# A hybrid layer on one core: when the conditioning products run in the mixer, and narrower products in the first feed-forward block

## The chip, the cores and the metric

One core of one Trainium2 chip runs the whole layer in one launch. The metric is the time on the device of one execution. The kernel before took 543.53 us (median of 3 runs, 543.39 to 544.7). The profiled execution took 542.25 us, of which the profile's span covers 540.5 us.

## The reference

One decoder layer on 256 tokens with 1024 features, in float32. The input x passes a SwiGLU feed-forward block, a mixer and a second feed-forward block, each with a normed and modulated input and a gated residual, and a last norm.

```
mod = (c @ w_ada + b_ada).reshape(B, 9, 1024)
sh1, sc1, g1, sh2, sc2, g2, sh3, sc3, g3 = [mod[:, None, i] for i in range(9)]
h = rmsnorm(x, ffn1_norm) * (1 + sc1) + sh1
x = x + 0.5 * (1 + g1) * swiglu(h, ffn1_w_gate, ffn1_w_up, ffn1_w_down)
h = rmsnorm(x, mix_norm) * (1 + sc2) + sh2
x = x + (1 + g2) * hybrid_mixer(h, ...)
h = rmsnorm(x, ffn2_norm) * (1 + sc3) + sh3
x = x + 0.5 * (1 + g3) * swiglu(h, ffn2_w_gate, ffn2_w_up, ffn2_w_down)
return rmsnorm(x, final_norm)
```

swiglu(h) is (silu(h @ w_gate) * (h @ w_up)) @ w_down with a hidden width of 2816. The mixer projects h to q, k, v of an attention with 8 heads, to x_m for a stabilised mLSTM with 4 heads (in the reference in chunks of 64 tokens), and to a gate z. It norms both results, multiplies the mLSTM's by silu(z), and multiplies the two, side by side, by w_out. The nine vectors of mod are the conditioning: 9 x 1024 sums over 1024 elements, one for each feature and kind.

## The kernel before, in words

Features lie on the partitions and the 256 tokens along the free axis. A product in float32 is made from two parts of each operand: `hi` is the value rounded to TensorE's fp32r format, `lo` the remainder. `mm3` issues three matmuls of 256 columns (258 where two columns for the shift are carried along): hi by hi, lo weight by hi, hi weight by lo. Weights come in pieces of 1 MB (`raw`, 4 buffers); ScalarE (ACT) makes `whi` of a piece by a cast, VectorE (DVE) makes `wlo` by a subtraction, each in two halves of 1024 columns. `weights()` hands out one piece, asks for the one three ahead, and splits the next.

The conditioning is not made by TensorE. For each of the 72 rows of 128 features `ada` loads 512 KB (3 buffers) and DVE multiplies it by c and sums along the row: one `scalar_tensor_tensor`, called `junk` in the trace after its unused output. `side(...)` is called at fixed places and takes one such job from the list `jobs` for each of its arguments. After the first feed-forward block 22 jobs are left for the mixer: 6 for the mixer's gate, 8 for the scale of the third norm and 8 for its shift.

The work goes in this order. The first feed-forward block makes gate and up until 140.5 us and the down product until about 202 us: 8 output blocks d, each over 22 pieces of the hidden width. In it, one matmul of 512 columns takes hi of a weight block against [gh|gl], the two halves of the hidden values, and a second of 256 columns takes lo against gh. The second half of the 512 lands in its own part of the PSUM tile, and DVE adds it to x with a `scalar_tensor_tensor` (`x` in the trace) of its own. The second block's down product is made in the same way for d = 0 to 6, and by `mm3` for the last d.

The mixer runs from 202 to 340 us: x_m (`px`), then pairs of column tiles in `tiles()`: queries 0 and 1, values 0, queries 2 and 3, values 1, and z twice (each 16 `mm3`, in two halves). Between the tiles stand the small pieces of attention and mLSTM. `gates` and `decays` make the mLSTM's decay matrices `wE` (DVE, from a TensorE product of `rows` with `ohr`), `m_scores(h)` makes q by k and multiplies it into `wE[h]` on DVE, `m_sums` sums over it, `m_vars` and `m_factors` make the norm (`dd`, `vv`, `rs`, `nw`, `rows`), and `z_silu` is the silu of z. Then `w_out` in 4 pieces of weights c, each for two of the eight input tiles k: k = 0 to 3 is the attention's output (`mix(0)` to `mix(3)`, split into `hh` and `hl` from `oa`), k = 4 to 7 the mLSTM's, made in `m_out`. `pre_shift(2)` makes the two shift columns for the second feed-forward block, whose gate and up run from 340 to 468 us, the down product until 529 us.

The order on each engine comes from two sources. Instructions for which `keep_in_program_order` was called (through the class `Ordered`, while its `on` is set) keep the order of the code among themselves. All others are placed by the scheduler, which plays the program with its own costs and puts each where its engine seems free. In the mixer, ACT and DVE are pinned from `weigh(3)` to `a_out`, and from `m_factors` to `m_out_pre`; the conditioning products aren't. All DMAs of weights and rows are issued by SyncE (SP), in one queue. Almost every instruction has line 55 in the trace, that of the helper.

Of the kernel before, what the change touches and what calls it, by code (L numbers as in the profile page):

```python
# [14 lines left out]
ALU = mybir.AluOpType  # L15
# [5 lines left out]
ND = 8  # L21
# [40 lines left out]
def layer(ctx: ExitStack, tc: tile.TileContext, i, out: bass.AP):  # L62
    nc = tc.nc
    act, dve, pool, pe = (Ordered(tc, e) for e in (nc.scalar, nc.vector, nc.gpsimd, nc.tensor))
# [20 lines left out]
    def bank(tag):  # L85
        return psp.tile([P, 512], F32, tag=tag, name=nm("ps" + tag), bufs=BANKS[tag])
# [38 lines left out]
    c_bc = const([P, D], F32, "c_bc")  # L125
# [115 lines left out]
    mod = const([P, 72], F32, "mod")  # L241
# [2 lines left out]
    gt = [const([P, ND], F32, f"gt{k}") for k in range(3)]  # L244
    NCOL = [C_N1, C_N2, C_N3]

    def ada(col, on_pool=False):

        t = wp.tile([P, D], F32, tag="ada", name=nm("ada"), bufs=3)
        dma(t, i["ada"][col])  # L250
        junk = wp.tile([P, D], BF16, tag="junk", name=nm("junk"), bufs=1)
        dve.scalar_tensor_tensor(junk, t, 1.0, c_bc, ALU.mult, ALU.mult,
                                 accum_out=mod[:, col:col + 1])

    def ada_gate_fin(k):
        s0 = 24 * k + 16
# [145 lines left out]
    def ffn(k, nxt):  # L402
        nfa = 3
        with tc.tile_pool(name=f"g{k}", bufs=1) as gp:
# [132 lines left out]
            for d in range(ND):  # L537
                pd = bank(ring[d % 8])
                for ft in range(NF):
                    b = d * NF + ft  # L540
                    if b % 16 == 0:
                        w = weights()
                        side(*QD[k][b // 16 % 2])
                    if nxt is None and d == ND - 1:
                        mm3(pd[:, 0:T], w, (b % 16) * P, gh[:, ft], gl[:, ft], start=(ft == 0), stop=(ft == NF - 1))
                        continue
                    hi, lo = part(w, (b % 16) * P, P)
                    pe.matmul(pd, hi, g2[:, ft], start=(ft == 0), stop=(ft == NF - 1), skip_group_check=True)
                    rest.append(lambda lo=lo, ft=ft, pd=pd: pe.matmul(
                        pd[:, 0:T], lo, gh[:, ft], start=False, stop=(ft == NF - 1), skip_group_check=True))  # L550
                    while rest and (ft < NF - 4 or ft == NF - 1):
                        rest.pop(0)()
                if nxt is not None or d < ND - 1:
                    dve.scalar_tensor_tensor(x_sb[:, d], pd[:, T:2 * T], gt[k][:, d:d + 1], x_sb[:, d], ALU.mult,
                                             ALU.add)
                nxt_sq[0] = residual(d, pd[:, 0:T], gt[k], nxt)
                if d == 6 and nxt is not None:
                    pre_shift(nxt)
# [5 lines left out]
    def side(*on):  # L564

        for o in on:
            if jobs:
                jobs.pop(0)(o)
# [5 lines left out]


    px = [bank("a") for _ in range(4)]
    for c in range(2):
        w = weights()
        side(1, 0)
        for d4 in range(4):  # L580
            d = c * 4 + d4
            for h in range(NH):
                mm3(px[h][:, 0:W], w, d4 * 512 + h * P, hh[:, d], hl[:, d], start=(d == 0), stop=(d == 7))
            if d == 0:
                r = rstd_of([acc, nxt_sq[0]], pre=False)
    with tc.tile_pool(name="mix", bufs=1) as mp:
        mixer(tc, nc, i, mp, locals())


    with tc.tile_pool(name="fin", bufs=1) as fp:  # L590
# [10 lines left out]
def mixer(tc, nc, i, mp, L):  # L601
    act, dve, pool, pe, sp = L["act"], L["dve"], L["pool"], L["pe"], L["sp"]
# [221 lines left out]
    def mix(k):  # L824
        return mix0 if k == 0 else (hh[:, k, 0:T], hl[:, k, 0:T])
# [3 lines left out]
    def z_silu(h2):  # L829
        z2 = zs[:, 2 * h2:2 * h2 + 2]  # L830
        tc.keep_in_program_order(act.activation(z2, z2, AF.Silu))
# [105 lines left out]
    conv(1)  # L937
    next(g)
    fold()
    side(1, 0)  # L940
    g = queries(1)
    conv(2)
    next(g)
    conv(3)
    next(g)
    g0 = values(0)
    side(0, 1)
    next(g0)
    gates()
    next(g0)  # L950
    scores(0)
    m_queries()
    g = queries(2)
    side(0, 1)
    next(g)
    next(g0)
    m_values()
# [2 lines left out]
    scores(1)  # L960
    turn(0)
    g = queries(3)
    side(0, 1)
    next(g)
    weigh(0)
    m_scores(0)
# [3 lines left out]
    scores(2)  # L970
    m_scores(2)
    g0 = values(1)
    side(0, 1)
    next(g0)
    weigh(1)
    scores(3)
# [3 lines left out]
    m_scores(3)  # L980
    m_sums(1)
    g = tiles(shifted(zs[:, 0]), shifted(zs[:, 1]))
    side(1, 0, 0)
    next(g)
    next(g0)
    turn(3)
# [10 lines left out]
    m_vars(1)  # L997
    m_vars(2)
    g = tiles(shifted(zs[:, 2]), shifted(zs[:, 3]))
    side(1)  # L1000
    next(g)
    m_vars(3)
    m_factors()
    z_silu(0)
    next(g)
    for j in range(1, 4):
        hilo(*mix(j), oa[:, j, 0:T])
    z_silu(1)
    for h in range(NH):
        m_out_pre(h)  # L1010
# [1 line left out]
    po = [bank(t) for t in ("m", "m", "a", "a")]  # L1012
    for c in range(4):
        w = weights()
        side(0)
        pe.on = c < 2
        for k2 in range(2):
            k = c * 2 + k2
            for d in range(8):
                mm3(po[d // 2][:, (d % 2) * T:(d % 2 + 1) * T], w, (k2 * 8 + d) * P, *mix(k),  # L1020
                    start=(c == 0 and k2 == 0 and d % 2 == 0), stop=(c == 3 and k2 == 1))
                if (k, d) == (2, 7):
                    m_spread()
                    for h in range(NH):
                        m_out(h)
    side(*[0] * len(jobs))
    L["pre_shift"](2)
    for d in range(8):
        nxt_sq[0] = residual(d, po[d // 2][:, (d % 2) * T:(d % 2 + 1) * T], L["gt"][1], 2)

# [85 lines left out]
```

## Time and profile before

| | us |
|---|---|
| time, median of 3 runs | 543.53 |
| time of the profiled execution | 542.25 |
| span of the profile | 540.5 |
| TensorE (PE) busy | 516.9 (96%), 3826 matmuls |
| VectorE (DVE) busy | 424.1 (78%) |
| ScalarE (ACT) busy | 282.6 (52%) |
| DMA | 125.73 MB, mean 233 GB/s |
| PE idle in one piece, in the mixer | 4.20 before 282.05, 0.74 before 285.74, 4.75 before 316.55 |

Busy time is the sum of the instructions of an engine, with overlaps counted once. An idle time in brackets stands ahead of the instruction that ended it, with the engine that released it. "PEclk" is the granted clock of TensorE as a share of full speed. In the chain of waits each row is one stretch of the path that ended last.

### The profile page before, as it was taken

How to read it: one execution, taken by the hardware profiler on the slowest of the kernel's cores; microseconds unless marked ns; L12 is line 12 of the kernel's file. 1: busy time of each engine (PE TensorE's matmuls, PEld its weight loads, DVE VectorE, ACT ScalarE, POOL GpSimd, SP SyncE). 2: the span in 40 equal slices, each digit the busy share in tenths (PEclk: the TensorE clock that was granted, in tenths of full speed). 3: DMA queues.
4: the chain of work that ended last, by engine and by line, in shares of the span. 5: the costliest groups of instructions: out<-in, count | busy, mean ns of one | idle time of the engine just before them, and what ended most of it. 6: DMA issues, size and time to landing. Idle time of an engine off the chain costs nothing.

```text
span 540.5 us, 9607 instructions
## 1 busy us (share of the span) xinstructions
PE 516.9 (96%) x3826; PEld 484.0 (90%) x3826; DVE 424.1 (78%) x717; ACT 282.6 (52%) x484; POOL 46.2 (9%) x60
## 2 busy tenths in 40 slices
PE   8999999999999999999969969999999999999992
PEld 7899999999988889978856869999999999988892
DVE  7899978988799988997894666979987777655433
ACT  4364456665554454648655544965554554544410
POOL 5000000000010210200010000400000000012320
PEclk9999999999999999999999979999999999999997
DMA  8999986587788985776771114387855455455002
GB/s 314 352 368 396 372 333 235 212 303 276 278 345 320 346 340 180 266 297 235 308 275 42 50 69 136 101 349 292 312 202 206 178 169 211 167 181 209 1 1 78
DMA packets 24095, 125.73 MB, mean 233 GB/s; under 512 B 2673, under 2 KB 3185, under 8 KB 14578
## 3 DMA queue, kind: packets, MB, share of 16 engines
q1 hardware_dynamic: 23762, 124.72, 61.6%
q8 instruction: 30, 0.49, 0.4%
q10 hardware_dynamic: 288, 0.39, 0.2%
q14 instruction: 15, 0.12, 0.1%
HBM read 124.05 MB, written 1.05 MB: 231 GB/s over the span
## 4 chain that ended last, share of the span: by engine, by line
PE 89%; DVE 4%; DMA 2%; ACT 2%; issue 1%; SPq 0%; DVEq 0%; ACTq 0%
PE psa L55 45%; PE psb L55 25%; PE psm L55 20%; DMA ada<-in_ada 2%; DVE junk L55 1%; ACT whi L55 1%; DVE wE L55 1%; DVE wlo L55 0%; DVE ht L55 0%; DVE u_out L55 0%; SPq L98 0%; ACT hh L55 0%; ACT L55 0%; ACT zs L55 0%; DVE nw L55 0%
## 5 line engine op out<-in xcount | busy, mean ns | idle before, releaser
L55 ACT ACTIVATE whi<-raw 128x1024 fp32r<-128x1024 f32 (+1 forms) x160 | 166.8, 1047 | 133.1 <-PE psa L55 83.4
L55 DVE TENSOR_TENSOR wlo<-raw,whi 128x1024 fp32r<-128x1024 f32 (+1 forms) x160 | 193.8, 1215 | 50.3 <-ACT whi L55 48.7
L55 PE MATMUL psa<-hh,wlo 128*128 128x256 f32 (+1 forms) x452 | 127.2, 282 | 0.0
L55 PE MATMUL psa<-hh,whi 128*128 128x256 f32 (+1 forms) x452 | 127.0, 283 | 0.0
L55 PE MATMUL psa<-hl,whi 128*128 128x256 f32 (+1 forms) x452 | 126.1, 281 | 0.0
L55 DVE SCALAR_TENSOR_TENSOR junk<-ada,c_bc 128x1024 bf16<-128x1024 f32 x72 | 89.4, 1242 | 8.3 <-DMA ada<-in_ada 7.7
L55 PEld LDWEIGHTS psa<-hh,wlo 128*128 128x128 f32 x452 | 85.9, 190 | 0.1
L55 PEld LDWEIGHTS psa<-hh,whi 128*128 128x128 f32 x452 | 85.7, 190 | 0.0
L55 PEld LDWEIGHTS psa<-hl,whi 128*128 128x128 f32 x452 | 85.5, 190 | 0.0
L55 PE MATMUL psb<-hh,whi 128*128 128x258 f32 (+1 forms) x284 | 81.6, 288 | 0.6 <-ACT whi L55 0.6
L55 PE MATMUL psb<-hh,wlo 128*128 128x258 f32 (+1 forms) x284 | 80.2, 283 | 0.6 <-DVE wlo L55 0.6
L55 PE MATMUL psb<-hl,whi 128*128 128x258 f32 (+1 forms) x284 | 79.8, 283 | 0.0
L55 PE MATMUL psa<-g,whi 128*128 128x512 f32 (+1 forms) x198 | 59.8, 369 | 0.0
L55 PEld LDWEIGHTS psb<-hh,whi 128*128 128x128 f32 x284 | 53.7, 189 | 2.7 <-issue 1.0
L55 PEld LDWEIGHTS psb<-hh,wlo 128*128 128x128 f32 x284 | 53.8, 189 | 0.9 <-DVE wlo L55 0.8
L55 PEld LDWEIGHTS psb<-hl,whi 128*128 128x128 f32 x284 | 53.5, 189 | 0.2 <-issue 0.2
L55 PE MATMUL psm<-hh,whi 128*128 128x256 f32 (+1 forms) x168 | 48.1, 287 | 4.8 <-ACT hh L55 4.8
L55 PE MATMUL psm<-hh,wlo 128*128 128x256 f32 (+1 forms) x168 | 47.8, 285 | 0.0
L55 PE MATMUL psm<-hl,whi 128*128 128x256 f32 (+1 forms) x168 | 47.5, 285 | 0.0
L55 PE MATMUL psa<-g,wlo 128*128 128x256 f32 x176 | 45.9, 281 | 0.0
L55 PEld LDWEIGHTS psa<-g,whi 128*128 128x128 f32 x198 | 35.2, 188 | 6.2
L55 PEld LDWEIGHTS psm<-hh,whi 128*128 128x128 f32 x168 | 32.5, 194 | 5.1 <-ACT hh L55 5.0
(238 smaller groups left out, 759.5 us busy)
## 6 DMA issues: line engine op xcount, KB each, us to landing
ada<-in_ada SPq DMA_DIRECT2D x72, 512.0 KB, 5.8
raw<-in_dn SPq DMA_DIRECT2D x22, 1024.0 KB, 4.8
raw<-in_guB SPq DMA_DIRECT2D x19, 1024.0 KB, 4.8
raw<-in_gu SPq DMA_DIRECT2D x18, 1024.0 KB, 6.4
raw<-in_gu SPq DMA_DIRECT2D x8, 512.0 KB, 7.3
raw<-in_wqk SPq DMA_DIRECT2D x4, 1024.0 KB, 5.4
raw<-in_wout SPq DMA_DIRECT2D x4, 1024.0 KB, 6.8
raw<-in_guA SPq DMA_DIRECT2D x4, 768.0 KB, 4.0
```

The source lines that it names most:

```text
L55: r = f(*a, **k)
```

## The change

There are five edits. While `pinned[0]` is set, from the end of the first feed-forward block to the end of the mixer, the conditioning products are kept in program order with the other pinned instructions of DVE. Their places in the mixer are dealt out anew: 2 and 1 in x_m, 2 in the first queries, one each in the five pairs of tiles that follow, 5 in the first z pair, 4 in the second, 2 and 1 in the last two pieces of w_out (before: two in each place up to values 1, then 3, 1, 1, 1). `z_silu(0)` moves behind the splits of `mix(1)` to `mix(3)`. `pre_shift(2)` is pinned on ACT and DVE. In the down product of the first feed-forward block all eight output blocks are made by `mm3`, and the DVE add of the second half falls away there; the second feed-forward block keeps the 512 columns.

```diff
+    pinned = [False]
+
     def ada(col, on_pool=False):
 
         t = wp.tile([P, D], F32, tag="ada", name=nm("ada"), bufs=3)
         dma(t, i["ada"][col])
         junk = wp.tile([P, D], BF16, tag="junk", name=nm("junk"), bufs=1)
-        dve.scalar_tensor_tensor(junk, t, 1.0, c_bc, ALU.mult, ALU.mult,
-                                 accum_out=mod[:, col:col + 1])
+        p = dve.scalar_tensor_tensor(junk, t, 1.0, c_bc, ALU.mult, ALU.mult, accum_out=mod[:, col:col + 1])
+        if pinned[0]:
+            tc.keep_in_program_order(p)
...
-                    if nxt is None and d == ND - 1:
+                    if nxt is not None or d == ND - 1:
                         mm3(pd[:, 0:T], w, (b % 16) * P, gh[:, ft], gl[:, ft], start=(ft == 0), stop=(ft == NF - 1))
                         continue
...
-                if nxt is not None or d < ND - 1:
+                if nxt is None and d < ND - 1:
                     dve.scalar_tensor_tensor(x_sb[:, d], pd[:, T:2 * T], gt[k][:, d:d + 1], x_sb[:, d], ALU.mult,
                                              ALU.add)
...
     px = [bank("a") for _ in range(4)]
+    pinned[0] = True
     for c in range(2):
         w = weights()
-        side(1, 0)
+        side(*[0] * (2 - c))
...
     g = tiles(shifted(zs[:, 0]), shifted(zs[:, 1]))
-    side(1, 0, 0)
+    side(0, 0, 0, 0, 0)
...
     g = tiles(shifted(zs[:, 2]), shifted(zs[:, 3]))
-    side(1)
+    side(0, 0, 0, 0)
     next(g)
     m_vars(3)
     m_factors()
-    z_silu(0)
     next(g)
     for j in range(1, 4):
         hilo(*mix(j), oa[:, j, 0:T])
+    z_silu(0)
     z_silu(1)
...
-        side(0)
+        side(*[0] * c if c > 1 else ())
...
     side(*[0] * len(jobs))
+    act.on = dve.on = True
     L["pre_shift"](2)
+    act.on = dve.on = False
```

Between the lines shown, five calls of `side` in the tiles lose their second argument: queries 1, 2 and 3 and values 0 and 1.

The first place is DVE ahead of the decay matrices. Before, these rows stood in a row there (`raw_3256` is the first piece of w_out, `mx` belongs to the attention's scores, `ht` to the first z pair):

```order
L55 SCALAR_TENSOR_TENSOR junk_3406,mod<-ada_3404,c_bc 128x1024
L55 TENSOR_TENSOR em_2872<-nM_2868,F_2864 4x256
L55 TENSOR_TENSOR rows_2545<-nM_2868,rows_2545 4x256
L55 TENSOR_REDUCE mx_3315<-psa_3305 128x1 x2
L55 TENSOR_SCALAR mx_3224<-mx_3224 128x4
L55 TENSOR_TENSOR ht_3445<-rr_2420,psb_3418 128x256
L55 TENSOR_REDUCE mx_3315<-psa_3306 128x1 x2
L55 SCALAR_TENSOR_TENSOR junk_3551,mod<-ada_3549,c_bc 128x1024
L55 TENSOR_TENSOR wlo_3560<-raw_3256,whi_3559 128x1024
L55 TENSOR_SCALAR em_2872<-em_2872 4x256
L55 SCALAR_TENSOR_TENSOR wE_394_2550<-psm_3014,nac_2549,maskt 128x256
```

After the change it reads so (`raw_3104` is the first z pair's piece, `pr` belongs to the attention):

```order
L55 TENSOR_TENSOR rows_2709<-nM_3024,rows_2709 4x256
L55 TENSOR_SCALAR em_3028<-em_3028 4x256
L55 TENSOR_SCALAR mx_3224<-mx_3224 128x4
L55 COPY nac_2713<-psm_3162 128x8
L55 RECIPROCAL ri_3232<-su_3231 128x4
L55 TENSOR_SCALAR pr_3230<-pr_3230,ri_3232 128x128
L55 TENSOR_SCALAR pr_3230<-pr_3230,ri_3232 128x256
L55 TENSOR_SCALAR pr_3230<-pr_3230,ri_3232 128x128
L55 TENSOR_SCALAR pr_3230<-pr_3230,ri_3232 128x256
L55 SCALAR_TENSOR_TENSOR junk_3258,mod<-ada_3256,c_bc 128x1024
L55 SCALAR_TENSOR_TENSOR wE_392_2714<-psm_3166,nac_2713,maskt 128x256
L55 SCALAR_TENSOR_TENSOR wE_392_2714<-psm_3166,nac_2713,maskt 128x128
```

Now `wE` comes ahead of all splits of w_out, with one conditioning product just ahead of it; before, two products and a split of w_out's first piece stood in these rows alone. Of the 22 products of the mixer, 20 stood ahead of the first `wE` in DVE's order before, and 9 do now.

The second place is the end of the second z pair, on DVE, where `rows` and the splits `hl` wait for `m_factors`. Before (`raw_3553` is the third piece of w_out, `sh_155` the shift of the third norm):

```order
L55 TENSOR_TENSOR wlo_3665<-raw_3408,whi_3664 128x1024
L55 TENSOR_TENSOR dd_3594<-dd_3594,em_2872 4x256
L55 SCALAR_TENSOR_TENSOR vv_3597<-psa_3333,dd_3594 4x256
L55 TENSOR_TENSOR hl<-sh_155,hh 128x8 x2
L55 TENSOR_TENSOR wlo_3723<-raw_3553,whi_3722 128x1024
L55 SCALAR_TENSOR_TENSOR nw_3602<-rs_3599 4x256
L55 SCALAR_TENSOR_TENSOR nw_3602<-vv_3597,nw_3602 4x256
L55 SCALAR_TENSOR_TENSOR rs_3599<-nw_3602,rs_3599 4x256
L55 TENSOR_TENSOR wlo_3727<-raw_3553,whi_3726 128x1024
L55 TENSOR_TENSOR rows_2545<-rs_3599,rows_2545 4x256
L55 TENSOR_TENSOR ht_3636<-rr_2420,psb_3609 128x256
```

After:

```order
L55 SCALAR_TENSOR_TENSOR junk_3707,mod<-ada_3705,c_bc 128x1024
L55 TENSOR_TENSOR wlo_3829<-raw_3560,whi_3828 128x1024
L55 TENSOR_TENSOR dd_3758<-dd_3758,em_3028 4x256
L55 SCALAR_TENSOR_TENSOR junk_3711,mod<-ada_3709,c_bc 128x1024
L55 SCALAR_TENSOR_TENSOR vv_3761<-psa_3474,dd_3758 4x256
L55 SCALAR_TENSOR_TENSOR junk_3715,mod<-ada_3713,c_bc 128x1024
L55 SCALAR_TENSOR_TENSOR nw_3766<-rs_3763 4x256
L55 SCALAR_TENSOR_TENSOR nw_3766<-vv_3761,nw_3766 4x256
L55 SCALAR_TENSOR_TENSOR rs_3763<-nw_3766,rs_3763 4x256
L55 TENSOR_TENSOR wlo_3883<-raw_3717,whi_3882 128x1024
L55 TENSOR_TENSOR wlo_3887<-raw_3717,whi_3886 128x1024
L55 TENSOR_TENSOR rows_2709<-rs_3763,rows_2709 4x256
```

Three of the four products of the second z pair stand among the pinned steps of `m_factors` (the first of the four is just ahead of these rows), and both halves of the split of w_out's third piece (now `raw_3717`) stand ahead of `rows`. The shift's two `hl` went to the end of w_out.

On ACT at the same place, before:

```order
L55 ACTIVATE whi_3726<-raw_3553 128x1024
L55 ACTIVATE rows_2545<-rs_3599 4x256
L55 ACT_TABLE_LOAD
L55 ACTIVATE zs_2557<-zs_2557 128x512
L55 ACTIVATE col_3634<-psb_3609 128x1
L55 ACTIVATE zs_2557<-ht_3636,col_3634 128x256
L55 ACTIVATE hh<-oa_2559 128x256 x3
L55 ACTIVATE zs_2557<-zs_2557 128x512
```

After:

```order
L55 ACTIVATE whi_3882<-raw_3717 128x1024
L55 ACTIVATE whi_3886<-raw_3717 128x1024
L55 ACTIVATE rows_2709<-rs_3763 4x256
L55 ACTIVATE col_3797<-psb_3772 128x1
L55 ACTIVATE zs_2721<-ht_3799,col_3797 128x256
L55 ACTIVATE hh<-oa_2723 128x256 x3
L55 ACT_TABLE_LOAD
L55 ACTIVATE zs_2721<-zs_2721 128x512 x2
```

The table load and the first silu went behind the three `hh` of `oa`.

The third place is SP's queue of transfers, from the z pairs on. Before:

```order
L98 DMA ada_3396<-in_ada 128x1024
L98 DMA ada_3400<-in_ada 128x1024
L98 DMA ada_3404<-in_ada 128x1024
L98 DMA raw_3408<-in_wout 128x2048
L98 DMA ada_3549<-in_ada 128x1024
L98 DMA raw_3553<-in_wout 128x2048
L98 DMA raw_3658<-in_wout 128x2048
L98 DMA ada_3668<-in_ada 128x1024
L98 DMA raw_3720<-in_guA 128x1536
```

After (from the second piece of w_out on):

```order
L98 DMA raw_3560<-in_wout 128x2048
L98 DMA ada_3701<-in_ada 128x1024
L98 DMA ada_3705<-in_ada 128x1024
L98 DMA ada_3709<-in_ada 128x1024
L98 DMA ada_3713<-in_ada 128x1024
L98 DMA raw_3717<-in_wout 128x2048
L98 DMA raw_3822<-in_wout 128x2048
L98 DMA raw_3880<-in_guA 128x1536
L98 DMA raw_3964<-in_guA 128x1536
L98 DMA ada_3974<-in_ada 128x1024
```

Four rows of conditioning now stand ahead of the third piece of w_out; before there was one, and three ahead of the second piece.

## Rows read from the trace of the kernel before

**Rows 1.** The page, parts 1, 4: busy time of TensorE; chain by engine.

```profile
PE 516.9 (96%) x3826; PEld 484.0 (90%) x3826; DVE 424.1 (78%) x717; ACT 282.6 (52%) x484; POOL 46.2 (9%) x60
...
PE 89%; DVE 4%; DMA 2%; ACT 2%; issue 1%; SPq 0%; DVEq 0%; ACTq 0%
```

**Rows 2.** Windows of four stretches of the mixer.

```profile
core 0: us, PE busy (x) PEld busy (x) DVE busy (x) ACT busy (x) POOL busy (x), PEclk, DMA share, GB/s
262.00:277.80 15.80, 15.80 (x122) 13.39 (x120) 15.06 (x33) 8.16 (x18) 1.55 (x1) 1.00 0.79 306
290.00:300.00 10.00, 10.00 (x70) 7.99 (x70) 2.31 (x5) 4.80 (x13) 0.72 (x1) 1.00 0.01 2
300.00:311.50 11.50, 11.50 (x85) 9.76 (x85) 7.11 (x14) 6.37 (x15) 0.00 (x0) 1.00 0.19 69
316.60:323.00 6.40, 6.40 (x31) 6.40 (x32) 4.19 (x11) 1.93 (x4) 0.00 (x0) 0.52 0.14 54
```

**Rows 3.** Timeline of PE, from 282 (start, length, what; idle before).

```profile
282.05 2.95 PE L55 MATMUL psm<-qk,xc 128*128 128x256 f32 x8 [4.20 <-DVE wE L55]
...
285.74 0.92 PE L55 MATMUL psm<-qk,xc 128*128 128x256 f32 x4 [0.74 <-DVE wE L55]
```

**Rows 4.** Timeline of DVE in the same place.

```profile
278.15 1.22 DVE L55 SCALAR_TENSOR_TENSOR junk<-ada,c_bc 128x1024 bf16<-128x1024 f32 x1
...
279.29 1.23 DVE L55 TENSOR_TENSOR wlo<-raw,whi 128x1024 fp32r<-128x1024 f32 x1
...
280.62 2.67 DVE L55 SCALAR_TENSOR_TENSOR wE<-psm,nac,maskt 128x256 f32<-128x256 f32 x8
```

**Rows 5.** The page, part 5: the ada products (72).

```profile
L55 DVE SCALAR_TENSOR_TENSOR junk<-ada,c_bc 128x1024 bf16<-128x1024 f32 x72 | 89.4, 1242 | 8.3 <-DMA ada<-in_ada 7.7
```

**Rows 6.** Timeline of PE in the output product.

```profile
316.55 0.58 PE L55 MATMUL psm<-hh,whi 128*128 128x256 f32 x1 [4.75 <-ACT hh L55]
```

**Rows 7.** Timeline of ACT before that matmul.

```profile
313.21 1.28 ACT L55 ACT_TABLE_LOAD   x1
314.50 0.63 ACT L55 ACTIVATE zs<-zs 128x512 f32<-128x512 f32 x1
315.04 0.15 ACT L55 ACTIVATE col<-psb 128x1 f32<-128x1 f32 x1
316.10 1.01 ACT L55 ACTIVATE hh<-oa 128x256 fp32r<-128x256 f32 x3
```

**Rows 8.** Timeline of DVE before that matmul.

```profile
311.27 0.40 DVE L55 SCALAR_TENSOR_TENSOR nw<-rs 4x256 f32<-4x256 f32 x1
...
312.92 1.23 DVE L55 TENSOR_TENSOR wlo<-raw,whi 128x1024 fp32r<-128x1024 f32 x1 [0.35 <-ACT whi L55]
...
315.23 0.42 DVE L55 TENSOR_TENSOR ht<-rr,psb 128x256 f32<-128x256 f32 x1 [0.64 <-ACT col L55]
```

**Rows 9.** Transfers of 262 to 272: count, size, time to landing.

```profile
raw<-in_wout SPq DMA_DIRECT2D x3, 1024.0 KB, 7.2
ada<-in_ada SPq DMA_DIRECT2D x3, 512.0 KB, 3.8
```

**Rows 10.** Chain of waits, down products of both feed-forward blocks.

```profile
156.04 15.40 PE psa L55 x88
...
506.23 7.76 PE psm L55 x44
...
513.99 15.46 PE psa L55 x110
```

**Rows 11.** Down products, first block: weight loads; the add that goes.

```profile
L55 PEld LDWEIGHTS psa<-g,whi 128*128 128x128 f32 x88 | 16.2, 188 | 3.6
...
L55 DVE SCALAR_TENSOR_TENSOR x<-psa,gt,x 128x256 f32<-128x256 f32 x6 | 2.9, 477 | 0.0
```

**Rows 12.** Timeline of DVE, second half of the output product.

```profile
328.85 0.76 DVE L55 TENSOR_TENSOR hl<-ht,hh 128x256 fp32r<-128x256 f32 x2
```

**Rows 13.** Timeline of PE there.

```profile
328.69 0.28 PE L55 MATMUL psm<-hh,whi 128*128 128x256 f32 x1
```

More of the change, by code (lines that the diff above doesn't have):

```diff
@@ L587, in layer @@
         mixer(tc, nc, i, mp, locals())
+    pinned[0] = False
     with tc.tile_pool(name="fin", bufs=1) as fp:
@@ L939, in mixer @@
     fold()
-    side(1, 0)
+    side(0)
     g = queries(1)
@@ L946, in mixer @@
     g0 = values(0)
-    side(0, 1)
+    side(0)
     next(g0)
@@ L953, in mixer @@
     g = queries(2)
-    side(0, 1)
+    side(0)
     next(g)
@@ L962, in mixer @@
     g = queries(3)
-    side(0, 1)
+    side(0)
     next(g)
@@ L972, in mixer @@
     g0 = values(1)
-    side(0, 1)
+    side(0)
     next(g0)
```

## The prediction

> **What bounds the kernel now.** I read the page first: TensorE is busy for 516.9 of the 540.5 us and holds 89% of the chain that ended last [rows 1]. So time is to be had where TensorE stands idle, or where its products take more engine time than they must. The timeline of PE shows that its long idle pieces all lie in the mixer, and that there are two places.
>
> Place A is at 278 to 286. TensorE waits 4.20 us for the `wE` of DVE, runs four pairs of `m_scores` matmuls in 2.95 us, and waits 0.74 us again [rows 3]. The next four matmuls take 0.92, so the eight would take 1.84 at the same rate; the other 1.1 is the clock, which is granted lower just after the idle piece. Place A costs 4.20 + 0.74 + 1.1 = 6.0 us. What holds DVE is seen in its own timeline: a conditioning product of 1.22 and a split of 1.23 stand right ahead of the 2.67 of `wE` [rows 4]. And they do so because DVE is full before: 15.06 of the 15.8 us up to there are busy [rows 2].
>
> Place B is in the output product. TensorE has used up `mix(0)` at 311.8 and waits 4.75 us for `hh` of ACT until 316.55 [rows 6]. After that its clock is 0.52 from 316.6 to 323, and 31 matmuls take 6.40 us, 206 ns each [rows 2]. At full clock a matmul of 256 columns takes 117 ns: the last 110 of the second block's down product took 15.46 us, 44 of them belong to a block that takes 7.76, and 66 of 256 columns in the other 7.70 make 117 ns each [rows 10]. Place B thus costs 4.75 + 31 x 0.089 = 7.5 us. The chain to it is `m_factors`: `nw` at 311.27, a split at 312.92 that waits 0.35 for ACT, `ht` at 315.23 that waits 0.64 for `col` of ACT [rows 8], and on ACT the table load 313.21 and silu 314.50 ahead of `col` 315.04 and `hh` 316.10 [rows 7].
>
> **The change part by part.**
>
> Down product of the first block. Per hidden piece, 512 + 256 columns in two matmuls become three of 256: 176 matmuls and 176 weight loads more, the same columns. The second block's last d is already made so, with the 66 matmuls in 7.70 us of above. The first block's own wide ones took 15.40 for two d, 7.70 each. Eight times the difference is between 8 x (7.70 - 7.76) = -0.5 and 0. I take -0.2. The 188 ns weight loads [rows 11] stay hidden, for the 117 ns period above contains them. The eight `x` adds of 0.48 that go [rows 11] lie beside TensorE and count nothing in the stretch itself.
>
> The Trainium skill, "TensorE: Matmul & The Clock Gate", Part 2 (Back-to-back issue gap), gives N / 2.4 + 2.5 ns for a lone matmul. By that, an estimate, three of 256 would take 327.5 ns where 512 + 256 take 325, and the 176 pieces would add 0.4 us. The rows have 350 and 353 per piece and so the other sign; no run yet shows these products in the first block.
>
> Place A. Ahead of the first `wE` stand 9 of the mixer's 22 products now, against 20. Eleven times 1.24 [rows 5] is 13.7 us less for DVE in a stretch where it was full. The decays' reading of `rows` also moves ahead of all splits of w_out, with tiles of projections behind it that TensorE can run meanwhile. The wait to be covered is 4.2 us, against 13.7 us removed, so I cost it as gone: -6.0. What is late next there is the attention's scores and `turn`, whose `pr` stand on the same DVE and gain as well. Bounds: 0 if the order ahead of `wE` waits for something else, -6.2 if the whole place runs at full clock.
>
> Products moved behind. Nine products go to the z pairs, 11.2 us of DVE. The windows from 290 to 311.5 leave 7.7 + 4.4 = 12.1 us of DVE idle [rows 2], so they just fit, if DVE takes them as they come. Five stand ahead of the attention's norm, in the free 7.7, and I cost them at nothing: TensorE is busy throughout there. Four stand among the pinned steps of `m_factors`. They are 5.0 us where DVE has 4.4 idle, 3.2 of it ahead of `nw` by my count along the timeline; being pinned, what doesn't fit delays `dd`, `vv`, `nw`, `rows`, then `ht` and the three `hl`, for which TensorE waits at B.
>
> Place B therefore has terms of both signs. The table load and the silu leave the way to `hh`: 1.28 + 0.63 [rows 7], but `ht` can then start no earlier than `rows` on DVE ends, 0.6 before its present 315.23; so -0.65, not -1.9. Pinned products push `nw` by about 0.3. And both halves of the split of w_out's third piece now stand ahead of `rows` on DVE, and their casts on ACT, pinned. That piece is asked for on SP behind four rows of conditioning, of which the last needs a buffer that the first of the four sets free (3 buffers), so behind that first product. Ahead of place A a piece of w_out took 7.2 us in a queue with others, a row of conditioning 3.8 [rows 9]. I count the first product done some 8.7 us into the second half of the first z pair (which begins at 296.75 before; B's wait ends 19.8 later), the piece landed at 14.5 to 16.2, then two casts and splits with `rows`, `ht`, `hh` behind: 20.1 to 21.4, against 19.8. So between +0.3 and +1.6; if the piece lands early the term falls to -0.65. I take +0.5. The lower clock behind it stays whatever it is (2.8 us now), and can move by 1.3 either way with the length of the wait.
>
> End of the mixer. Three products stand in the last two pieces of w_out. TensorE begins the mLSTM's inputs at 328.69 [rows 13] with eight matmuls that need only `hh`; at 117 ns they last until 329.6, and the first `hl` is made from 328.85 on [rows 12], just in time. One product of 1.24 stands ahead of `hl` now, so TensorE waits about 0.9. The x and `hl` at the start of the second block come behind the pinned shift: 0 to 0.7, I take 0.3. The two shift columns leave the way to B and gain what is in the -0.65.
>
> Sum: -0.2 - 6.0 + 0.5 + 0.9 + 0.3 = -4.5 us. The profiled execution of 542.25 us becomes 537.75; the median of the runs is 1.28 above that execution, so I predict 539.0 for the median.
>
> **The rivals.**
>
> Gain without the price, 0.25. The waits of the output product don't come, because DVE runs earlier all through the mixer once A is gone and the transfers land early: -0.2 - 6.2 - 0.65 and no more, 536.5. For it speaks that `m_factors` is at the end of a chain that A delays; against it that at B TensorE, not only DVE, came 6 us earlier.
>
> A wait in the place of A, 0.17. TensorE reaches B's inputs 6 us earlier and DVE, with as much work as before in the mixer, hasn't finished: the time moves to B and to a longer stretch at low clock. What decides is whether the nine moved products fit the idle 12.1 us: each one that doesn't costs 1.24. With four that don't, 5.0 of the gain are gone: 543.5, no change.
>
> Slower, 0.09. The third piece of w_out is the mechanism. SP's queue is in order, and the piece stands behind four rows and shares the engines with the fourth piece and the first of the second block asked for right behind it. Three pieces in flight took 7.2 us in the middle, longer for the last. From a landing of 16.1 us in my count on, each us late is one late at B, and a long wait costs clock behind it. To eat the 6.2 of A, it must land some 5 us later, at 21; with 2 us more and the waits of w_out it is 545.5. Against it: 300 to 311.5 moves only 69 GB/s now [rows 2].
>
> Weight loads in the open, 0.01. 176 more loads of 188 ns [rows 11] that TensorE doesn't hide would add 33 us, 572. The 117 ns period denies it. The Trainium skill, same page, Part 3 (The mechanism) says that a weight load overlaps a running matmul only where the row group differs, which is not so here; this case's trace does not agree, since 188 ns loads of full rows fit in 117 ns periods.
>
> **How the numbers follow.** The forecast, 537.5 to 541, has 0.48; the rivals 0.25, 0.17, 0.09 and 0.01. What a measurement of this kernel can tell from no change is about 0.3%, 1.6 us: faster is below 541.9. The forecast and the larger gain give 0.73, less 0.04 for a forecast that ends above 541.9, and a share of 0.02 of the second rival: 0.71 faster. Same gets 0.18, slower 0.11 from the third, fourth and part of the second. The range 535 to 544 leaves out the slow end and the largest gains, 2 in 10.
>
> **What would show it.** A right: no idle of TensorE over 1 us ahead of `m_scores`, the clock near 1.00 there. B right: one idle of 4.5 to 6.5 us ahead of the first `hh` of `oa`, released by ACT, with w_out's third piece landing about when DVE is done with `m_factors`. Output product right: a wait of about 1 us on `hl` just behind the first eight matmuls of k = 4. Down product right: blocks of 66 matmuls at 7.65 to 7.75 us. It is wrong if place A keeps a wait of 3 us or more, if B grows past 8 us, or if down blocks take more than 7.8 us.

## The result, and the profile after

The changed kernel took 536.79 us (median of 4, 536.74 to 537.58) against 543.61 us for the kernel before on the same chip (543.39 to 544.7): a ratio of 0.9874, with a 95% interval of 0.9857 to 0.9891. The profiled execution took 536.74 us with a span of 535.0. The forecast was 539.0 and, for the profiled execution, 537.75: the measured time lies in the range of 535 to 544, and just below the 537.5 to 541 that the forecast itself was given. The two traces stand 5.5 us apart, the medians 6.8; that difference is taken up in the part on the prediction.

The spans cut at the same matmuls, by the timeline of TensorE:

| stretch | before | after | difference | forecast |
|---|---|---|---|---|
| up to the first block's down product | 140.40 | 140.45 | +0.05 | |
| down product | 62.86 | 63.56 | +0.70 | -0.2 |
| mixer, to the last product of `mix(0)` | 108.25 | 100.78 | -7.47 | -6.0 |
| from there to the first product of `hh` (place B) | 5.04 | 5.02 | -0.02 | +0.5 |
| from there to `m_spread` | 8.63 | 7.95 | -0.68 | with the row above |
| `m_spread` to the second block | 14.87 | 15.82 | +0.95 | +0.9 |
| second block to the end | 200.45 | 201.42 | +0.97 | +0.3 |
| span | 540.5 | 535.0 | -5.5 | -4.5 |

Place A is gone. The four calls of `m_scores` (four matmuls each in the trace) stand far apart in the timeline of TensorE after the change, none behind a wait, and the granted clock is 1.00 throughout (start, length, engine, operation, in brackets the idle time ahead of it, where there is one):

```profile
264.61 0.87 PE L55 MATMUL psm<-qk,xc 128*128 128x256 f32 x4
...
266.26 0.82 PE L55 MATMUL psm<-qk,xc 128*128 128x256 f32 x4
...
269.75 0.92 PE L55 MATMUL psm<-qk,xc 128*128 128x256 f32 x4
...
278.03 0.82 PE L55 MATMUL psm<-qk,xc 128*128 128x256 f32 x4
```

Before, the first eight of these matmuls took 2.95 us behind 4.20 of idle time [rows 3], with a granted clock of 0.50 from 281.75 to 285.16. On DVE the one product that the order of the changed kernel shows ahead of the decays is still there, and the first `wE` begins at 259.85 instead of 280.62 [rows 4]:

```profile
258.71 1.22 DVE L55 SCALAR_TENSOR_TENSOR junk<-ada,c_bc 128x1024 bf16<-128x1024 f32 x1
...
259.85 1.39 DVE L55 SCALAR_TENSOR_TENSOR wE<-psm,nac,maskt 128x256 f32<-128x256 f32 x4
...
261.48 1.38 DVE L55 SCALAR_TENSOR_TENSOR wE<-psm,nac,maskt 128x256 f32<-128x256 f32 x4
```

If each matmul is counted from its start to the start of the next, the products of `rows` by `ohr` fall from 4.93 to 0.85 us and those of `m_scores` from 5.30 to 2.78, together 6.6 us. The other 0.9 us of the stretch lie spread over the small products of the attention, and that is what is left after a new wait of 0.60 us for `va` of ACT, ahead of `pT` by `va` at 285.67.

Place B is as long as before, and the chain of waits says what ends it (start, length, engine and tile):

```profile
297.46 1.16 DVE junk L55 x2
299.01 5.47 DMA raw<-in_wout
304.56 1.07 ACT whi L55
305.65 2.36 DVE wlo L55 x2
308.95 0.51 ACT zs L55
309.81 2.96 PE psm L55 x12
```

Two conditioning products, the transfer of w_out's third piece that SP could issue only behind them, its cast and split, then `zs` and `hh`. It is the chain of the prediction's third rival, with the piece landing at 299.01 + 5.47 = 304.48. The clock behind the wait (the column of 1.00, 0.80, ... is the granted clock, of 1.2 and 2.4 GHz the share of the upper one):

```profile
core 0: us, PE busy (x) PEld busy (x) DVE busy (x) ACT busy (x) POOL busy (x), PEclk, DMA share, GB/s
296.30:304.50 8.20, 8.20 (x67) 7.63 (x66) 7.97 (x17) 3.12 (x7) 0.00 (x0) 1.00 0.60 231
304.50:309.80 5.30, 0.57 (x5) 0.36 (x4) 4.29 (x8) 3.21 (x7) 0.00 (x0) 0.80 1.01 418
309.80:315.00 5.20, 5.19 (x26) 5.19 (x27) 3.74 (x10) 3.00 (x5) 0.00 (x0) 0.55 1.01 416
315.00:318.00 3.00, 3.00 (x26) 2.87 (x26) 1.83 (x3) 1.20 (x2) 0.00 (x0) 1.00 0.27 104
```

The lower clock (0.50) begins 2.2 us before the wait ends, at 307.63, and before the change it began 0.7 before that end, at 315.88. So less of it falls on the matmuls: 0.55 over 5.2 us with 26 matmuls, where before 31 ran at 0.52 in 6.40 us [rows 2]. By 315 it is over.

At the end of w_out DVE has a product ahead of the first `hl`, and TensorE runs out of `hh` for it:

```profile
321.10 1.22 DVE L55 SCALAR_TENSOR_TENSOR junk<-ada,c_bc 128x1024 bf16<-128x1024 f32 x1
...
322.58 0.75 DVE L55 TENSOR_TENSOR hl<-ht,hh 128x256 fp32r<-128x256 f32 x2
...
331.68 0.69 DVE L55 TENSOR_TENSOR wlo<-raw,whi 128x512 fp32r<-128x512 f32 x1 [0.75 <-ACT whi L55]
332.37 1.66 DVE L55 SCALAR_TENSOR_TENSOR x<-psm,gt,x 128x256 f32<-128x256 f32 x4
```

```profile
321.27 0.28 PE L55 MATMUL psm<-hh,whi 128*128 128x256 f32 x1
...
323.06 0.39 PE L55 MATMUL psm<-hl,whi 128*128 128x256 f32 x1 [0.68 <-DVE hl L55]
...
334.87 0.39 PE L55 MATMUL psa<-hh,whi 128*128 128x258 f32 x1 [0.16 <-DVE x L55]
...
335.63 0.51 PE L55 MATMUL psb<-hl,whi 128*128 128x258 f32 x2 [0.25 <-DVE hl L55]
```

The first row of TensorE is the first of eight products that need only `hh`; then comes a wait of 0.68 us for `hl`, which before was ready in time [rows 12, 13]. The `x` of the second block start at 332.37, behind a split, and two more short waits follow at the start of the second block.

The down product of the first block takes 7.81 us for 66 matmuls throughout (chain of waits: start, length, count):

```profile
140.61 7.81 PE psb L55 x66
...
156.23 15.62 PE psa L55 x132
```

Before, two blocks of 44 took 15.40 [rows 10].

### The profile page after: what moved, and what is told of

It is laid out like the page before. It is cut to its first block, busy times and chain, and to the rows that moved or that the text cites. A ratio compares the mean times of both kernels' runs of the same rounds, so it can differ in the third digit from the quotient of the medians.

```text
span 535.0 us, 9939 instructions
## 1 busy us (share of the span) xinstructions
PE 515.6 (96%) x4002; PEld 491.7 (92%) x4002; DVE 421.4 (79%) x709; ACT 281.9 (53%) x484; POOL 47.2 (9%) x60
## 4 chain that ended last, share of the span: by engine, by line
PE 87%; DVE 5%; DMA 3%; ACT 2%; issue 1%; SPq 1%; DVEq 0%; ACTq 0%
PE psa L55 44%; PE psb L55 24%; PE psm L55 19%; DVE junk L55 2%; DMA ada<-in_ada 2%; ACT whi L55 1%; DMA raw<-in_wout 1%; DVE wlo L55 1%; SPq L98 1%; DVE ht L55 1%; DVE x L55 1%; DVE u_out L55 0%; DVE hl L55 0%; ACT hh L55 0%; DVE oa L55 0%
## 5 line engine op out<-in xcount | busy, mean ns | idle before, releaser
L55 PE MATMUL psa<-g,whi 128*128 128x256 f32 (+1 forms) x286 | 61.8, 307 | 0.0
L55 PEld LDWEIGHTS psa<-g,whi 128*128 128x128 f32 x286 | 46.1, 188 | 2.7
L55 PE MATMUL psa<-g,wlo 128*128 128x256 f32 x176 | 47.9, 281 | 0.0
```

The source lines that it names most:

```text
L55: r = f(*a, **k)
```

## The experiments

All runs were compared with the kernel before on their chip. The changed kernel was not timed beside them, so a difference of a run's median from its 536.79 is the weaker evidence, and the stretches of the two traces the stronger. "Mixer" is the stretch of the table that was 108.25 before and 100.78 after the change, "wait" the one of 5.04 and 5.02. An "idle" wait is the number in brackets, 0.28 to 0.29 us shorter.

**The down product alone.**

```diff
-                    if nxt is not None or d == ND - 1:
+                    if nxt is None and d == ND - 1:
...
-                if nxt is None and d < ND - 1:
+                if nxt is not None or d < ND - 1:
```

> The changed kernel with the first feed-forward block's down product put back to 512 columns. Theory (the narrow products cost what the two traces show, 7.81 against 7.70 us for each of eight output blocks): 0.7 to 0.9 us less than the changed kernel, about 536.0 us, with the mixer as in the changed kernel. Rival 1 (the narrow products gain elsewhere, by taking eight adds off DVE before the mixer): no gain, 536.8 or more. Rival 2 (they save, as my prediction had it): 537.0.

535.91 us (535.71 to 537.22). The down product took 62.87 us, the mixer 100.86, the wait 5.00. The narrow products cost 0.7 us in the trace, as the theory had it, and 0.9 between the medians; the adds that they take off DVE give nothing back in the mixer.

**The dealing alone, and the pin alone.**

```diff
-    side(1, 0, 0)
+    side(0, 0, 0, 0, 0)
...
-        side(0)
+        side(*[0] * c if c > 1 else ())
```

> The kernel before with the products dealt out anew, but not pinned. Theory (place A is the number of products that stand on DVE ahead of the decay matrices, and without the pin 19 of 22 still stand there, against 9 in the changed kernel): the wait of 4 us before m_scores stays, 542 to 544 us. Rival (the dealing alone moves the transfers and with them the load; the pin is not needed): the wait goes, 537 to 539 us.

541.33 us (540.44 to 542.55), ratio 0.9955 (0.9935 to 0.9974). The rows are asked for later, yet the scheduler puts 19 of 22 products ahead of the decays, and place A stays, now as one wait:

```profile
281.24 4.34 PE L55 MATMUL psm<-qk,xc 128*128 128x256 f32 x12 [4.38 <-DVE wE L55]
```

The mixer took 107.5 us. The time is a little below the expected 542 to 544, the mechanism is as expected.

```diff
+        p = dve.scalar_tensor_tensor(junk, t, 1.0, c_bc, ...)
+        if pinned[0]:
+            tc.keep_in_program_order(p)
```

> The kernel before with the products pinned at their old places, 14 of 22 ahead of the decay matrices. Theory (load ahead of the decays decides, six products or 7.4 us less than before is more than the 4.2 us of wait): the wait before m_scores goes or falls under 1 us, and since the products of z stand where DVE is free, 537 to 539 us. Rival (only the new dealing makes room): the wait stays at over 2 us, 541 to 544 us.

536.65 us (535.34 to 536.92), ratio 0.9873 (0.9839 to 0.9908): the pin alone is worth as much as the whole change, and a little more than the expected 537 to 539. The wait ahead of `m_scores` is gone, the mixer took 102.4 us with 14 products ahead of the decays. It loses 1.6 us there against the changed kernel, and has 62.87 for the down product and 14.90 and 18.2 at the end, where the changed kernel has 15.82 and 19.2 (18.2 and 19.2 are the stretch from the second block's first product to its first whole tile). At place B the idle wait is 5.29 us, though the third piece lands at 293.30, before `mix(0)` is begun: a conditioning product stands between the split and `rows` on DVE there.

**The cause of place A, by itself.** Each of the 22 products sums over half of its elements here; the other half is left out.

```diff
+        n = D // 2 if half_on[0] else D
-        dve.scalar_tensor_tensor(junk, t, 1.0, c_bc, ALU.mult, ALU.mult,
+        dve.scalar_tensor_tensor(junk[:, 0:n], t[:, 0:n], 1.0, c_bc[:, 0:n], ALU.mult, ALU.mult,
```

> The kernel before, with each of the mixer's 22 conditioning products summed over 512 of its 1024 elements only (the other half of the sum is left out), so that each takes DVE about half the time; all transfers stay, nothing is pinned or dealt anew. Theory (DVE time ahead of the decay matrices makes place A): 16 products of about 0.65 us stand ahead of the first wE, as much DVE time as 8 of the full ones, so the wait before m_scores goes and the mixer up to mix(0) falls from 108.4 to 101 to 103 us. Rival (the place of the decays in the order, or the transfers of the rows, make it): a wait of over 2 us stays and the mixer takes 106 us or more.

534.32 us (533.52 to 534.63). Nothing is pinned or dealt anew, every transfer is there, and place A is gone; the mixer took 100.4 us:

```profile
263.18 0.82 PE L55 MATMUL psm<-qk,xc 128*128 128x256 f32 x4
...
266.34 0.82 PE L55 MATMUL psm<-qk,xc 128*128 128x256 f32 x4
...
269.39 0.92 PE L55 MATMUL psm<-qk,xc 128*128 128x256 f32 x4
```

So DVE's time ahead of the decays made place A, and not the transfers. (The scheduler knows the shorter length too, so the order isn't the old one in all places: 16 products stand ahead of the first `wE` instead of 20.)

**The third piece first.**

```diff
-    side(0, 0, 0, 0)
     next(g)
+    side(0, 0, 0, 0)
     m_vars(3)
```

> The changed kernel with the four products of the second z pair asked for behind that pair's weights, so that the third piece of w_out is transferred ahead of the four rows. Theory (the wait for hh before the second half of the first output piece ends with the landing of that piece): its casts start up to 3 us earlier, but the four products on DVE stay, and the wait falls from 4.7 to about 3.5 to 4.2 us: 535.5 to 536.5 us. Rival (the pinned products on DVE end it, the landing is just in time): the wait stays 4.7 us, 536.8 us.

539.39 us (539.15 to 540.02): 2.6 us slower than the changed kernel, and neither theory had it. The piece is early, but all four products now stand ahead of `dd`, where two did in the changed kernel, being pinned behind the tile instead of ahead of it. DVE is busy for 9.13 of the 9.20 us from 298.8 to 308, hardly more than in the changed kernel (9.09); it is the order that differs, and `dd` begins at 306.15 instead of 301.46:

```profile
305.01 1.22 DVE L55 SCALAR_TENSOR_TENSOR junk<-ada,c_bc 128x1024 bf16<-128x1024 f32 x1
...
306.15 0.41 DVE L55 TENSOR_TENSOR dd<-dd,em 4x256 f32<-4x256 f32 x1
...
311.19 0.42 DVE L55 TENSOR_TENSOR ht<-rr,psb 128x256 f32<-128x256 f32 x1
```

```profile
312.51 0.58 PE L55 MATMUL psm<-hh,whi 128*128 128x256 f32 x1 [7.44 <-ACT hh L55]
```

The idle time grew to 7.44 us: products that stand ahead of `dd` among the pinned steps of `m_factors` delay `hh`, and an earlier transfer is of no use behind them. This is a price such as the prediction's slower rival spoke of, reached by another way.

**No products in the second z pair.**

```diff
-    side(0, 0, 0, 0)
+    side(*[0] * 0)
```

with one more in queries 3 and values 1 and two more in the first z pair.

> The changed kernel with the four products of the second z pair moved forward, one each to queries 3 and values 1 and two to the first z pair; the three in w_out stay. Theory (these four hold the wait for hh at 4.7 us, by the third piece's late transfer and by DVE time among m_factors): the wait falls by 0.6, as the table load and silu gone from the way would give, or more, to 4.1 us or less, and the time to 535.5 to 536.2 us. Rival (the wait is set by the rest of the chain): 4.7 us and 536.8 us. Second rival (moved forward they bring the wait ahead of m_scores back): 538 us or more.

535.63 us (535.26 to 536.26). The wait fell from 5.02 to 4.43 us:

```profile
308.75 0.58 PE L55 MATMUL psm<-hh,whi 128*128 128x256 f32 x1 [4.15 <-ACT hh L55]
```

The third piece lands at 296.56 here, before `mix(0)` begins, so its transfer no longer counts. What is left is a chain that TensorE itself starts: the cast of the piece's second half waits for TensorE's last product of `mix(0)`, and the pinned split, `rows`, `ht`, `zs` and `hh` follow it:

```profile
304.64 1.06 ACT L55 ACTIVATE whi<-raw 128x1024 fp32r<-128x1024 f32 x1 [1.50 <-PE psa L55]
...
305.73 1.23 DVE L55 TENSOR_TENSOR wlo<-raw,whi 128x1024 fp32r<-128x1024 f32 x1 [0.42 <-ACT whi L55]
306.99 0.42 DVE L55 TENSOR_TENSOR rows<-rs,rows 4x256 fp32r<-4x256 f32 x1
307.43 0.42 DVE L55 TENSOR_TENSOR ht<-rr,psb 128x256 f32<-128x256 f32 x1
```

No run of the study has a shorter wait than these 4.15 us; two others without products in the second z pair have the same. The mixer took 100.0 us, so moving them forward did no harm. From `hh` to `m_spread` it took 8.55 us instead of 7.95: the lower clock began 0.9 us before the end of the wait instead of 2.2, and more of it fell on the matmuls (a granted clock of 0.66 over the stretch, against 0.71).

**No late products.**

```diff
-        side(*[0] * c if c > 1 else ())
```

with one more each in queries 3, values 1 and the first z pair.

> The changed kernel with the three products of w_out moved forward, one more each in queries 3, values 1 and the first z pair. Theory (each product that stands among the mLSTM's splits late in w_out delays hl and then the x of the second block: 0.95 us between m_spread and the second block, and 1.0 us at its start): both go, 1.5 to 2 us less than the changed kernel, 534.8 to 535.3 us. Rival (the 1.0 us at the start is the pinned shift's or the narrower products', and only the 0.95 goes): 535.9 us.

534.83 us (534.7 to 534.93), ratio 0.9837 (0.9806 to 0.9867). From `m_spread` to the second block 14.97 us, from there to the first whole tile 18.16: both losses are gone but for 0.1 us. The three late products cost 0.85 + 1.0 us, and the narrow products and the pinned shift, which are still there, have next to no part in it.

**The silu back.**

```diff
+    z_silu(0)
     next(g)
...
-    z_silu(0)
     z_silu(1)
```

> The changed kernel with z_silu(0) back ahead of the splits of mix(1) to mix(3). Theory (my prediction): table load and silu stand on the way to hh again; with the third piece landing late the way is set by rows on DVE, so 0.5 to 1.2 us more than the changed kernel, 537.3 to 538 us. Rival (they lie in ACT's time of waiting for DVE, and cost nothing): 536.8 us.

537.39 us (536.46 to 537.71). The wait grew from 5.02 to 5.40 us, less than the 0.65 of the prediction. In the trace the shorter low clock behind it (7.20 us to `m_spread`, against 7.95) gives back more than this. The median is 0.6 us above the changed kernel's, but the range (536.46 to 537.71) takes in all of that kernel's (536.74 to 537.58). So 0.4 us of wait is shown, and no difference in the time.

**Putting the gains together.** The changed kernel with 512 columns, the shift not pinned, and all seven products of the second z pair and w_out moved forward, also into queries 2:

> The changed kernel with the down product back at 512 columns, the shift not pinned, and all seven products of the second z pair and w_out moved forward (queries 2 and 3 one more each, values 1 two, first z pair three). Theory, if the costs add: 536.8 - 0.7 (narrow products) - 1.9 (late products) - 0.6 (wait) = 533.6 us. Rival (products moved forward fill DVE ahead of the scores again): a new wait before m_scores or a_out, 535.5 us or more.

535.46 us (534.44 to 536.4), where 533.6 was forecast. The wait is 4.43 us and the end is as short as hoped, but the mixer took 102.85 us, 2 us more than in the changed kernel, with 1.0 us of waiting for `ht` and the rest in small products of the attention. So a new wait came, as the rival had it, though not ahead of `m_scores`.

The next three have 512 columns and no late products, and leave four, two and none in the second z pair.

> The changed kernel with the down product back at 512 columns and the three products of w_out moved forward as in the run without late ones (queries 3, values 1, first z pair). Theory (the two gains add): 534.83 - 0.7 = 534.1 us. Rival (the order that the scheduler makes of the small attention products eats it, as in the run with all products moved): 535 us or more.

534.17 us (533.99 to 535.45), ratio 0.9842 (0.9811 to 0.9873): with the run without late products this is the fastest kernel of the study that makes all sums, below both kernels of the case. The down product gives 0.7 us. The idle wait is longer than in that run, 5.78 instead of 4.74 us, since the third piece lands 3.48 us after the first product of `mix(0)` instead of 2.44, and its casts wait for it:

```profile
304.52 2.00 ACT L55 ACTIVATE whi<-raw 128x1024 fp32r<-128x1024 f32 x2 [0.73 <-DMA raw<-in_wout]
...
308.90 0.51 ACT L55 ACTIVATE zs<-ht,col 128x256 f32<-128x256 f32 x1 [2.02 <-DVE ht L55]
```

> As the run before, with two of the second z pair's four products moved to the first. Theory (the wait for hh falls from 4.9 towards the 4.3 it had without those products): 533.6 to 534.0 us. Rival (the lower clock behind the wait begins later when the wait is shorter and gives it back, as the 9.0 against 8.6 us from hh to m_spread showed): 534.1 us.

536.57 us (535.55 to 536.96). Both expectations failed: the idle wait stayed at 5.8 us and a new one of 1.2 us for `ht` came in the second z pair. The transfer isn't what holds place B here: the third piece lands at 302.36, before `mix(0)` begins, and in the chain of waits `nw`, `rs` and `rows` of `m_factors` come behind the split. (The 9.0 and 8.6 of the expectation count to a later matmul of `m_spread`; to the first it is 8.55 and 8.34.)

> As the run before, with all four moved to the first z pair, which then has ten. Theory (wait 4.3 us): 533.5 to 533.9 us. Rival (ten products are 12.4 us of DVE in the first z pair and delay the attention's norm and its mix(0), for which w_out waits): a new wait, 535 us or more.

539.57 us (537.08 to 540.73). The rival was right in the time, and the wait of 4.15 us at place B is as the theory had it. Ten products are more than the first z pair has room for, and DVE waits for their rows too. Behind them `ht` is late, and TensorE waits 3.39 us for it in the second z pair, which comes ahead of `mix(0)`:

```profile
294.13 1.23 DVE L55 SCALAR_TENSOR_TENSOR junk<-ada,c_bc 128x1024 bf16<-128x1024 f32 x1 [0.76 <-DMA ada<-in_ada]
...
298.35 1.23 DVE L55 SCALAR_TENSOR_TENSOR junk<-ada,c_bc 128x1024 bf16<-128x1024 f32 x1 [1.10 <-DMA ada<-in_ada]
...
301.02 0.75 DVE L55 TENSOR_TENSOR ht<-rr,psb 128x256 f32<-128x256 f32 x2
```

```profile
301.49 0.39 PE L55 MATMUL psb<-hh,whi 128*128 128x258 f32 x1 [3.39 <-DVE ht L55]
```

## Why the prediction came out as it did

The direction and the main mechanism were right. The sum was made of five steps. It came nearer than its terms: against the forecast the traces have 1.5 us more gain at place A and 1.2 more at place B and behind it, and 0.9 and 0.7 less at the down product and in the second block, so that misses of both signs partly cancel. That part is luck.

*Place A, -6.0.* The wait and the lower clock behind it were worth 6.6 us by the matmuls' own periods, and the whole stretch 7.47. That the cause was DVE's time is shown by the run with half products (100.4 us of mixer with no other edit), and that the pin and not the dealing does it by the two runs of the parts. The prediction didn't separate these; it took from the order that 11 products leave, which was so, but would have been so with the pin alone in a lesser degree (6 leave, which is enough).

*Place B, +0.5.* It came out at -0.02, and -0.68 for the stretch behind it. My count had the piece landing 2.5 to 4.2 us after the first product of `mix(0)` (14.5 to 16.2 from 12.0 us before it). It landed 2.44 after it (304.48 against 302.04), the early end, and the wait then ends when it did. The mechanism (transfer behind the products, pinned split ahead of `rows`) is in the chain of waits row by row. The two terms can be told apart by the run without products in the second z pair, where the piece is early: 4.15 us of idle wait, against 4.75 before, so that the way without table load and silu gained 0.60 (forecast 0.65), and the late piece took 0.59 of it back (4.74). The 0.68 was inside the 1.3 that I allowed for the clock.

*End of the mixer, +0.9 and +0.3.* The first measured 0.95, and the run without late products took 0.85 away. The wait for `hl` in it is 0.68, where I had 0.9. The second was 0.97 instead of 0.3: I had counted the `x` as delayed a little by the pinned shift, and that run, with the shift still pinned, shows that the late products cause it. By the rows they stand ahead of the splits, and the `x` behind those.

*The down product, -0.2.* This step failed, in sign too: +0.70, and the 7.81 us of a block are past the 7.8 that I had named as a sign of being wrong. I had 66 narrow matmuls at 15.46 - 7.76 = 7.70 us, and 7.76 was the length of another block of 44. The row of the chain begins at 513.99, when the matmul before it has ended; the block's own first matmul begins earlier, and the timeline of the kernel before has the seam:

```profile
513.83 0.39 PE L55 MATMUL psa<-g,whi 128*128 128x512 f32 x1
...
521.00 0.63 PE L55 MATMUL psa<-g,wlo 128*128 128x256 f32 x4
521.47 0.28 PE L55 MATMUL psa<-g,whi 128*128 128x256 f32 x1
521.58 0.28 PE L55 MATMUL psa<-g,wlo 128*128 128x256 f32 x1
```

The narrow products begin at 521.47, so the 44 ahead of them took 7.64 from start to start (7.48 from 513.99) and not 7.76, and the next matmul of another tile follows at 529.27: 7.80 us for the 66. That is what each block of the first down product then took. So 66 narrow ones take 118.3 ns each and three of them 355, against 350 for the wide and the narrow one. The Trainium skill, "TensorE: Matmul & The Clock Gate", Part 2 (Back-to-back issue gap), has a fixed cost for each matmul in its formula for a lone one, from which I had estimated +0.4 for the 176 pieces. The traces agree in the sign, and have 0.7.

*Trace against median.* I added 1.28 us to go from the profiled execution to the median. For the kernel before that holds; the changed kernel's execution in the profile (536.74) is next to its median (536.79). Beside the experiments the kernel before was timed 35 times: in 26 runs the mean granted clock was 0.975 to 0.980 and the time 543.39 to 545.29 us, in 9 it was 0.983 to 0.986 and 540.74 to 542.22. The profiled execution of before had 0.985. The changed kernel has 0.988 or 0.989 in all four. So the median of before holds more lower clock than its trace showed; in the trace with the dealing alone twelve `m_scores` matmuls took 4.34 us behind the wait, while in that of before only the first eight ran so slowly (2.95). That the lower clock of those 26 runs lies at place A is likely from this, and not shown, for they have no trace.

The rivals: the larger gain without the price (536.5) came nearest in time, nearer than the forecast, but for other reasons than it gave: the waits of the output product did come. The wait in the place of A (543.5) didn't come in this kernel; waits for `ht` came in three that moved still more products forward, with the limit the prediction named, the room on DVE in the z pairs. The slower one needed the third piece at 21 us in my count; it landed at 14.4. Weight loads in the open (572) are refuted by 118.3 ns for each matmul with its load.

## What to carry to other kernels

Where a scheduler may place filler work freely, look at what it puts ahead of the step on which the bounding engine waits next. Pinning the filler in program order was worth the whole gain here, dealing it out anew without the pin about a third by the medians (ratios of 0.9873 and 0.9955), and less by the traces (spans of 539.2 against 540.5 before, and 533.6 with the pin). Filler that is pinned behind, among the steps of a chain for which the bounding engine waits, can cost its length there (in the run with the pin alone, one product behind the split makes the wait at place B 1.14 us longer than the 4.15 without it); count it against the idle time of that stretch, and the transfers that its buffers hold back with it. Where a wait does not fall below a certain length however the filler is dealt, look whether the bounding engine itself starts the chain that it waits for, as at place B.

A price taken from a row of a grouped view needs the seam checked in the timeline: a difference of two rows is wrong by as much as their borders are off, and by as much as one block differs from the next.

## What the runs showed that was not expected

The small products of the attention cost TensorE different times in different orders, without any wait in the profile: counted from start to start, the 32 of `ka` by `qa` took 6.15 us before, 5.14 after, and 4.30 in the run with all seven moved, while those of `pT` by `va` took 4.01, 3.74 and 4.65. The pin alone has 1.6 us more of mixer than the changed kernel, and no longer wait in it. This is one part of why the gains of the single parts did not add up, beside the new waits for `ht`. What decides it was not tried.

How much of the lower clock falls on the matmuls behind place B is not fixed by the length of the wait. With idle waits of 4.15, 4.74, 4.74 and 5.12 us (no products in z, no late ones, the changed kernel, the silu back) the stretch from `hh` to `m_spread` took 8.55, 8.34, 7.95 and 7.20 us, at granted clocks of 0.66, 0.68, 0.71 and 0.79. In these four the clock gave back part of what the wait cost or more. But the kernel before, with 4.75, took 8.63 us at 0.64, and the run with the third piece first, with 7.44, took 8.03 at 0.71. So the stretch goes with the granted clock, and a change of the wait by half a us can be undone in it.
